# Large tiles moved to multiples of 512 bytes, and the heads' small pool divided in two, in a one-core encoder layer

## The chip, the cores and the metric

The kernel runs on one core of a Trainium2 chip. The metric is device time in microseconds of one execution; 0.2% of it is 3.1 us. A core has TensorE (PE, with its weight loads shown apart as PEld), VectorE (DVE), ScalarE (ACT), GpSimd (POOL) and SyncE (SP), which here issues most DMAs. SBUF is the on-chip memory: 128 partitions, and a tile takes the same bytes at the same address in each of them.

## What is computed

One layer over 1024 tokens of width 1024, all in float32:

```python
h = rmsnorm(x, g_mix)
z = h @ w_in                      # 512 pooling channels | q | k | v, 8 heads
y_pool = pool_mixer(u_pool, w_pool_grp, pool_scale)      # trailing windows 2, 4, 8, 16
y_attn = diff_attention(q, k, v, g_q, g_k, lam, g_sub, lambda_init)   # two softmax maps a head
gates = sigmoid(h @ w_gate + b_gate)
merged = gates[:, :1024] * (y_pool @ w_branch_pool) + gates[:, 1024:] * (y_attn @ w_branch_attn)
x = x + merged @ w_out
h2 = rmsnorm(x, g_ffn)
x = x + square(relu(h2 @ w_up)) @ w_down                 # width 4096 between
```

## The kernel before

**Three matmuls for one.** Every operand is split into a high and a low part in the type fp32r (split, L117): ScalarE copies the value, rounded, into the high part, and VectorE or GpSimd subtracts it from the value into the low part. mm3 (L122) then does hi x hi (L125), hi x lo (L126) and lo x hi (L127). In `matmul(ps, lhs, rhs)` the first operand, lhs, is loaded as weights (128 x 128, so 512 bytes in each partition), and rhs is the one that moves, 512 columns (2048 bytes), or 384, 256 or 128. Nearly every matmul has its own load of weights.

**The stages, in order of time.** The heads (L299 to L674): x is normed and transposed into hT; for each head and each block of 128 tokens, z = hT x wqkv (384 columns), then the preparation of queries and keys, transposes against the identity matrix (L469, L565), the scores sc from Q (weights) and K (moving, L509 and L510), the softmax, its transposed digits AT, and their product with the values, po, and two small products with a matrix of ones (L600, L601). The gates g and the pooling channels u, yp (L677 to L773), computed from hT, are placed by the framework's scheduler between the heads' matmuls. Then the pooling branch bp (L816 to L825), the attention branch ba (L827 to L846), the output projection op (L884), the second norm, and the MLP. The MLP is done with the Strassen-Winograd scheme: w_up in 16 pairs of column blocks, each with seven products of 12 matmuls (up_pair, L1050: X, Y, Z, W from B11, B21, BT1 to BT4 and B22), and w_down in seven products of 192 matmuls (d_product, L1242: Da and Db from u as weights and w moving).

**What sets the order.** Each engine runs its instructions in one fixed order. The framework's scheduler settles it when the program is built, from priorities and its own timeline; loads go out through SP's queue in that order.

**What sets the addresses.** Each `tile_pool` is a stretch of every partition; pools are stacked from the left in the order in which they are opened, or from the right (`side="right"`), and within a pool the tiles follow each other, each rounded up to 32 bytes. The left stack begins at byte 16512. const (L86) lies first and holds the identity identf (512 bytes), mhalf (32), ones (512), inv (64), cols (128) and six more of 32: 1440 bytes. So everything stacked after it begins at 17952, which is 35 x 512 + 32. All tiles from there on are multiples of 512 bytes long, up to the two of fo_tile (L141, 528 floats, 2112 bytes each): after these, fq and up begin at 160 past a multiple of 512. sp (L300), the heads' pool, holds large and small tiles in one: a few of 4 to 64 bytes, then dist, the square sq, qn, the queries' digits Q, oS and oqs. Pools from the right begin at 229344, which is 447 x 512 + 480.

Of the kernel before, what the change touches and what calls it, by code (L numbers as in the profile page):

```python
# [8 lines left out]
F32 = mybir.dt.float32  # L9
F32R = mybir.dt.float32r  # L10
# [7 lines left out]
P = 128  # L18
S = 1024
# [14 lines left out]
N_FW, N_FR, N_FO = 4, 2, 2  # L34
N_Q, N_QN = 3, 2
# [22 lines left out]
def encoder_kernel(  # L58
# [21 lines left out]
    nc = tc.nc  # L80
# [3 lines left out]
    w_up, w_down, w_pool_grp = w_up[0], w_down[0], w_pool_grp[0]  # L84

    const = ctx.enter_context(tc.tile_pool(name="const", bufs=1))  # L86
    dram = ctx.enter_context(tc.tile_pool(name="dram", bufs=1, space=DRAM))
    mix = ctx.enter_context(ExitStack())
    hp0 = [mix.enter_context(tc.tile_pool(name=f"hp0{i}", bufs=4)) for i in "ab"]
# [3 lines left out]
    fp = mix.enter_context(tc.tile_pool(name="fp", bufs=1))  # L93
# [8 lines left out]
    def htile(shape, dt, name, th):  # L102

        if th == 0:
            hcount[0] += 1
        return (hp1 if th else hp0[(hcount[0] - 1) // 4 % 2]).tile(shape, dt, tag="H", name=name)
# [7 lines left out]
    def f(ap):  # L114
        return ap.bitcast(F32)
# [23 lines left out]
        return wpool.tile(shape, F32R, tag="fw", name=name, bufs=N_FW)  # L139

    def fo_tile(name):  # L141
        return fp.tile([P, 528], F32, tag="fo", name=name, bufs=N_FO)

    def fr_tile(shape, name):
        return fp.tile(shape, F32, tag="fr", name=name, bufs=N_FR)
# [88 lines left out]
        mp.append(m)  # L234


    identf = const.tile([P, P], F32, name="identf")
    make_identity(nc, identf)
    mhalf = const.tile([P, NT], F32, name="mhalf")
    nc.gpsimd.memset(mhalf, -0.5)  # L240
    ones = const.tile([P, P], F32R, name="ones")
    nc.gpsimd.memset(f(ones), 1.0)
    inv = const.tile([P, 16], F32, name="inv")
    for i in range(16):
        nc.gpsimd.memset(inv[:, i : i + 1], 1.0 / (i + 1))

    cols = const.tile([P, 32], F32, name="cols")
    gs = const.tile([P, 1], F32, name="gs")
    zero = const.tile([P, 1], F32, name="zero")
    y_dram = dram.tile([D, S], F32, name="y_dram")  # L250
# [10 lines left out]
    def norm_transpose(xt, gb, t, dst, hn, small, banks, halves=False):  # L261

        th, c0 = t // 4, (t % 4) * P
        ss = small.tile([P, 1], F32, tag="ss", name=f"ss{t}", bufs=2)
        rs = small.tile([P, 1], F32, tag="rs", name=f"rs{t}", bufs=2)
        if halves:
            s1 = small.tile([P, 1], F32, tag="ss1", name=f"ss1{t}")
            nc.scalar.activation(hn[:, 0:512], xt[:, 0:512], AF.Square, accum_out=ss)
            nc.vector.tensor_tensor_reduce(
                out=hn[:, 512:D], in0=xt[:, 512:D], in1=xt[:, 512:D],  # L270
                scale=1.0, scalar=D * EPS, op0=ALU.mult, op1=ALU.add, accum_out=s1,
            )
            nc.vector.tensor_scalar(rs, s1, ss, 1.0 / D, op0=ALU.add, op1=ALU.mult)
            nc.gpsimd.tensor_tensor(rs, rs, mhalf[:, 0:1], op=ALU.pow)
        else:
            nc.scalar.activation(hn, xt, AF.Square, accum_out=ss)
            rsq(rs, ss, 1, 1.0 / D)
        for j in range(2):
            js = slice(j * 512, (j + 1) * 512)
            nc.vector.scalar_tensor_tensor(hn[:, js], xt[:, js], rs, gb[:, js], op0=ALU.mult, op1=ALU.mult)  # L280
            trp, trtag = banks[j % len(banks)]
            ps = trp.tile([P, 512], F32, tag=trtag, name=f"hps{t}_{j}")
            for i in range(4):
                k = 4 * j + i
                nc.tensor.transpose(ps[:, i * P : (i + 1) * P], hn[:, k * P : (k + 1) * P], identf)
            for i in range(2):
                kp = 2 * j + i
                src = ps[:, i * 256 : (i + 1) * 256].rearrange("p (a b) -> p a b", a=2)
                split(dst[kp, th, 0][:, :, c0 : c0 + P], dst[kp, th, 1][:, :, c0 : c0 + P], src)
# [7 lines left out]


    with ExitStack() as ph:  # L299
        sp = ph.enter_context(tc.tile_pool(name="sp", bufs=1))  # L300
        ps_s = ph.enter_context(tc.tile_pool(name="ps_s", bufs=N_S, space=PSUM))
        ps_o = ph.enter_context(tc.tile_pool(name="ps_o", bufs=1, space=PSUM))
        ps_t = ph.enter_context(tc.tile_pool(name="ps_t", bufs=N_T, space=PSUM))

        def s1(shape, dt, name, tag, bufs=1):
            return sp.tile(shape, dt, tag=tag, name=name, bufs=bufs)

        xs = {}

# [70 lines left out]
        lqk = s1([P, 4, HD], F32, "lqk", "oq")  # L380
        nc.sync.dma_start(lqk, lambda_qk[0].partition_broadcast(P))

        dist = sp.tile([P, S], F32, name="dist")

        def distances():

# [5 lines left out]
        def columns():  # L392
            cols_ps = ps_t.tile([P, 512], F32, tag="tr", name="cols_ps")
            nc.tensor.transpose(cols_ps[:, 0:32], rows, identf[0:32, 0:32])
            nc.vector.tensor_copy(cols, cols_ps[:, 0:32])
            nc.vector.tensor_scalar(gs, cols[:, 20:21], 1.0 - LAMBDA_INIT, None, op0=ALU.mult)

        def small_params():
# [64 lines left out]
        def stage_qkT(h, t):  # L463

            th, c0 = t // 4, (t % 4) * P
            K, qn = KV[h][0][th], st[h, t]["qn"]
            tr = ps_t.tile([P, 512], F32, tag="tr", name=f"tk{h}_{t}")
            for i in range(2):
                nc.tensor.transpose(  # L469
                    tr[:, i * P : (i + 1) * P], qn[:, 2 * i : 2 * i + 2, :].rearrange("p a b -> p (a b)"), identf  # L470
                )
            Q = sp.tile([P, 2, 2, P], F32R, tag="Q", name=f"Q{h}_{t}", bufs=N_Q)
            halves = (slice(0, HD), slice(HD, P))
            for m in range(2):
                own, other = halves[m], halves[1 - m]
                q, k = tr[own, 0:P], tr[own, P : 2 * P]
                k_hi, q_hi = K[own, m, c0 : c0 + P], Q[own, m, 0, :]
                nc.scalar.copy(k_hi, k)
                nc.vector.tensor_tensor(K[other, m, c0 : c0 + P], k, f(k_hi), op=ALU.subtract)  # L479
                nc.scalar.copy(q_hi, q)  # L480
                nc.vector.tensor_tensor(Q[other, m, 0, :], q, f(q_hi), op=ALU.subtract)
                nc.vector.tensor_tensor(Q[own, m, 1, :], q, f(q_hi), op=ALU.subtract)  # L482
                nc.scalar.copy(Q[other, m, 1, :], q)  # L483
            st[h, t]["Q"] = Q
            yield

        def stage_scores(h, t):

            K, Q = KV[h][0], st[h, t]["Q"]
            n = (t + 1) * P  # L490
# [139 lines left out]
        def stage(w, g):  # L630
            h, t = divmod(g, NT)
            if w == "A":
                if t == 0:
                    head_start(h)
                yield from stage_qkv(h, t)
            elif w == "B":
                yield from stage_prep(h, t)
            elif w == "C":
                yield from stage_qkT(h, t)
            elif w == "D":  # L640
                yield from stage_scores(h, t)
            elif w == "E":
                yield from stage_aT(h, t)
            elif w == "F" and t % 2:
                yield from stage_pv(h, t // 2)
            elif w == "H" and t % 2:
                yield from stage_ssq(h, t // 2)
            elif w == "R" and t == NT - 1:
                yield from stage_norm(h)
            elif w == "W" and t == 0 and h:  # L650
                for kp in range(NK // 2):
                    load_w(h, kp)
                    split_w(h, kp, nc.gpsimd)
# [56 lines left out]
    def pool_group(g):  # L710
# [7 lines left out]
        for th in range(2):  # L718
# [7 lines left out]
            while sh < win:  # L726
                nxt = fo_tile(f"sum{g}_{th}_{sh}")
                nc.gpsimd.tensor_copy(nxt[:, 0:sh], cur[:, 0:sh])
                nc.vector.tensor_tensor(nxt[:, sh:n], cur[:, sh:n], cur[:, 0 : n - sh], op=ALU.add)
                cur = nxt  # L730
                sh *= 2
# [12 lines left out]
            ps = ps_f.tile([P, 512], F32, tag="f", name=f"yp{g}_{th}")  # L744
            mm3(ps, wg[:, 0, :], wg[:, 1, :], m[:, 0, :], m[:, 1, :], True, True)
            yp = fo_tile(f"yps{g}_{th}")
            nc.scalar.activation(yp[:, 0:512], ps, AF.Copy, scale=cols[:, 16 + g : 17 + g])
            nc.scalar.dma_start(p_dram[g * P : (g + 1) * P, th * 512 : (th + 1) * 512], yp[:, 0:512])

    def gate_cols(c):  # L750
        ws = fill_w(w_gate, c * P, f"gate{c}")
        for th in range(2):
            ps = fill_proj(ws, th, f"g{c}_{th}", spare_bank if c >= G_Z else fill_bank)
            fo = fo_tile(f"go{c}_{th}")
            nc.scalar.activation(fo[:, 0:512], ps, AF.Identity, bias=cols[:, c : c + 1])  # L755
            nc.scalar.dma_start(g_dram[c * P : (c + 1) * P, th * 512 : (th + 1) * 512], fo[:, 0:512])
            yield
# [69 lines left out]
    for d in range(NK):  # L827
# [10 lines left out]
        for th in range(2):  # L838
# [5 lines left out]
            t = htile([P, 2, 512], F32R, f"mT{d}_{th}", th)  # L844
# [9 lines left out]
    def pool_of(stack, name, bufs, space=None, side=None):  # L854
        kw = {} if space is None else {"space": space}
        return stack.enter_context(
            tc.tile_pool(name=name, bufs=bufs, reuse_waits="tile", side=side, **kw)
        )
# [7 lines left out]
    dve, pool = nc.vector, nc.gpsimd  # L866
    hs = ctx.enter_context(ExitStack())
    norms = ExitStack()
    nb_pool = pool_of(hs, "nb", 4, side="right")
    pr1 = pool_of(hs, "pr1", N_R1, side="right")  # L870
    pr2 = [pool_of(hs, "pr20", 1, side="right")]
# [460 lines left out]
```

## Time and profile before

| | us |
|---|---|
| median of 3 runs (1557.16 to 1557.71) | 1557.21 |
| the profiled execution's own time | 1556.93 |
| its span, first to last instruction | 1555.1 |
| TensorE busy, 7649 matmuls | 1535.1 |
| VectorE busy | 1012.4 |
| ScalarE busy | 816.0 |
| GpSimd busy | 350.2 |

By start time within the span: heads with gates and pooling channels up to 713 us, the pooling branch up to 746, the attention branch to 835, the output projection with the second norm to about 940, the up stage to 1243, the down stage to 1551. In a row of a view, `L125 PE MATMUL ba<-yT,wba 128*128 128x512` is line, engine, operation, what is written and what is read (the numbers of buffers left out), the array's rows and columns, and the size that moves. A matmul's start is measured, its end is modelled: rows overlap, since the next matmul starts while the one before still runs through the array.

### The profile page before, as it was taken

The numbers are of one execution on the slowest core, as the hardware profiler recorded it, in microseconds if no ns is written. First come the engines' busy times: TensorE is split into PE (matmuls) and PEld (weight loads), VectorE is DVE, ScalarE is ACT, GpSimd is POOL, SyncE is SP. The second block draws the span as 40 slices with busy tenths as digits, with TensorE's granted clock in tenths as the row PEclk, the third lists the DMA queues.
The fourth block names the chain that finished last, engine by engine and source line by source line (L and its number), as shares of the span: only waits on it lengthen the run. The fifth ranks groups of instructions, "written<-read, shape, count | busy, mean of one in ns | idle before, by whom it ended". The sixth has DMA issues, their size and how long they took to land.

```text
span 1555.1 us, 22054 instructions
## 1 busy us (share of the span) xinstructions
PE 1535.1 (99%) x7649; PEld 1321.5 (85%) x7649; DVE 1012.4 (65%) x2268; ACT 816.0 (52%) x1808; POOL 350.2 (23%) x447
## 2 busy tenths in 40 slices
PE   7999999999999999999999999999999999999999
PEld 6999999999998989888888887888888788888887
DVE  6777677777878787765322448766665668556662
ACT  6656556656566556566432456565555634333331
POOL 5433334243425262324453400000000000000000
PEclk9999999999999999999999999999999999999999
DMA  7111212021202031547426524554432789537750
GB/s 229 47 56 48 65 41 68 24 74 40 72 28 84 28 96 42 176 151 235 143 92 198 178 102 122 179 183 159 136 135 109 273 312 385 179 122 256 224 189 27
DMA packets 166681, 206.41 MB, mean 133 GB/s; under 512 B 10069, under 2 KB 102954, under 8 KB 166570
## 3 DMA queue, kind: packets, MB, share of 16 engines
q1 hardware_dynamic: 149162, 177.71, 35.3%
q10 hardware_dynamic: 17408, 27.30, 4.7%
q8 instruction: 60, 0.98, 0.3%
q14 instruction: 51, 0.42, 0.1%
HBM read 150.42 MB, written 54.56 MB: 132 GB/s over the span
## 4 chain that ended last, share of the span: by engine, by line
PE 89%; DVE 4%; issue 2%; DMA 2%; ACT 2%; POOL 1%; POOLq 0%; SPq 0%; ACTq 0%; DVEq 0%
PE z L125 5%; PE z L127 5%; PE z L126 5%; PE Da L126 4%; PE Da L125 4%; PE Da L127 4%; PE g L125 3%; PE g L126 3%; PE g L127 3%; PE Db L126 3%; PE Db L125 3%; PE Db L127 3%; PE X L125 2%; PE X L126 2%; PE X L127 2%; PE sc L509 2%
## 5 line engine op out<-in xcount | busy, mean ns | idle before, releaser
L125 PE MATMUL z<-wqkv,hT 128*128 128x384 f32 x512 | 174.9, 342 | 0.5 <-DVE qn L451 0.3
L127 PE MATMUL z<-wqkv,hT 128*128 128x384 f32 x512 | 174.7, 341 | 0.5 <-DVE hT L120 0.4
L126 PE MATMUL z<-wqkv,hT 128*128 128x384 f32 x512 | 174.0, 340 | 0.0
L520 ACT ACTIVATE s<-s,nm 128x256 f32<-128x256 f32 (+7 forms) x128 | 99.6, 778 | 45.4 <-DVE nm L512 40.7
L259 POOL TENSOR_TENSOR ms<-ms,mhalf 128x4 f32<-128x4 f32 x64 | 66.5, 1040 | 159.0 <-DVE ms L258 140.6
L126 PE MATMUL g<-hT,fwgate 128*128 128x512 f32 x256 | 101.1, 395 | 0.0
L125 PE MATMUL g<-hT,fwgate 128*128 128x512 f32 x256 | 101.0, 394 | 0.1
L127 PE MATMUL g<-hT,fwgate 128*128 128x512 f32 x256 | 101.0, 395 | 0.0
L125 PEld LDWEIGHTS z<-wqkv,hT 128*128 128x128 f32 x512 | 97.1, 190 | 4.3 <-DVE qn L451 1.0
L127 PEld LDWEIGHTS z<-wqkv,hT 128*128 128x128 f32 x512 | 96.9, 189 | 3.1 <-DVE hT L120 1.2
L126 PEld LDWEIGHTS z<-wqkv,hT 128*128 128x128 f32 x512 | 97.1, 190 | 2.9
L512 DVE CUSTOM_DVE_ANT_0 s<-sc,dist 128x512 f32<-128x512 f32 (+3 forms) x128 | 74.6, 586 | 19.5 <-PE sc L510 18.1
L120 POOL TENSOR_TENSOR wqkv<-rqkv,wqkv 128x384 fp32r<-128x384 f32 x60 | 63.7, 1078 | 19.8 <-ACT wqkv L119 19.8
L120 DVE TENSOR_TENSOR AS<-s,AS 128x512 fp32r<-128x512 f32 x64 | 43.9, 688 | 36.1 <-ACT AS L119 35.9
L509 PE MATMUL sc<-K,Q 128*128 128x512 f32 (+2 forms) x192 | 66.8, 354 | 0.1
L510 PE MATMUL sc<-K,Q 128*128 128x512 f32 (+2 forms) x192 | 66.4, 354 | 0.0
L457 POOL TENSOR_TENSOR qn<-qn,ggh 128x128 f32<-128x128 f32 x64 | 32.3, 505 | 138.7 <-DVE qn L451 127.6
L483 ACT CAST Q<-tk 64x128 fp32r<-64x128 f32 x128 | 33.2, 259 | 57.9 <-DVE Q L482 56.0
L480 ACT CAST Q<-tk 64x128 fp32r<-64x128 f32 x128 | 33.0, 258 | 53.5 <-DVE K L479 52.1
L120 POOL TENSOR_TENSOR fwgate<-frgate,fwgate 128x512 fp32r<-128x512 f32 x32 | 43.9, 1376 | 52.3 <-ACT fwgate L119 52.1
L127 PEld LDWEIGHTS g<-hT,fwgate 128*128 128x128 f32 x256 | 48.1, 188 | 8.7
L125 PEld LDWEIGHTS g<-hT,fwgate 128*128 128x128 f32 x256 | 48.2, 188 | 7.4 <-ACT go L755 0.4
(429 smaller groups left out, 4647.0 us busy)
## 6 DMA issues: line engine op xcount, KB each, us to landing
wd<-in_w_down_dram SPq DMA_DIRECT2D x56, 512.0 KB, 5.3
wu<-in_w_up_dram SPq DMA_DIRECT2D x32, 512.0 KB, 5.0
udS<-us SPq DMA_DIRECT2D x64, 256.0 KB, 2.2
ur<-udS SPq DMA_DIRECT2D x32, 512.0 KB, 3.5
rqkv<-in_w_in_dram SPq DMA_DIRECT2D x64, 192.0 KB, 2.8
ud<-u ACTq DMA_DIRECT2D x48, 256.0 KB, 2.9
ur<-ud SPq DMA_DIRECT2D x24, 512.0 KB, 4.9
frgate<-in_w_gate_dram SPq DMA_DIRECT2D x32, 256.0 KB, 2.8
```

Source lines behind the costliest of these rows:

```text
L120: (lo_eng or nc.vector).tensor_tensor(lo, src, f(hi), op=ALU.subtract)
L125: nc.tensor.matmul(ps, lhs_hi, rhs_hi, start=first, stop=False, **kw)
L126: nc.tensor.matmul(ps, lhs_hi, rhs_lo, start=False, stop=False, **kw)
L127: nc.tensor.matmul(ps, lhs_lo, rhs_hi, start=False, stop=last, **kw)
L259: nc.gpsimd.tensor_tensor(dst, dst, mhalf[:, :n], op=ALU.pow)
L457: nc.gpsimd.tensor_tensor(qn[:, 2:4, :], qn[:, 2:4, :], ggh.unsqueeze(1).broadcast_to([P, 2, HD]), op=ALU.mult)
L480: nc.scalar.copy(q_hi, q)
L483: nc.scalar.copy(Q[other, m, 1, :], q)
L509: nc.tensor.matmul(dst, Q[:, i, 0, :], rhs, start=True, stop=False)
L510: nc.tensor.matmul(dst, Q[:, i, 1, :], rhs, start=False, stop=True)
L512: nc.vector.tensor_tensor_reduce(out=s[i][:, c : c + w], in0=sc[:, 0:w], in1=dist[:, o0 + c : o0 + c + w], scale=2.0 ** -(h + 1), scalar=B ...
L520: nc.scalar.activation(s[i][:, 0:n], s[i][:, 0:n], AF.Exp, bias=last, scale=-1.0, accum_out=Z[:, i, t : t + 1])
```

## The change

Nothing is computed otherwise. The changed kernel moves where tiles begin:

- identf and ones leave const for a pool of their own, units, stacked behind it; cols shrinks from 32 to 24 columns (its last 11 were not read). const is then 384 bytes long and ends at 16896, which is 33 x 512; units adds 1024.
- fo_tile's tiles grow from 528 to 576 floats, so that two of them are 9 x 512 bytes.
- sp is divided: sq_pool takes the large tiles (lqk and oq, dist, sq, qn, Q, oS, oqs), sp keeps the small ones and is stacked behind it.
- a tile edge of 480 bytes, written once and never read, is put at the far right, so that the pools from the right begin at a multiple of 512.

```diff
+    units = ctx.enter_context(tc.tile_pool(name="units", bufs=1))
...
     def fo_tile(name):
-        return fp.tile([P, 528], F32, tag="fo", name=name, bufs=N_FO)
+        return fp.tile([P, 576], F32, tag="fo", name=name, bufs=N_FO)
...
-    identf = const.tile([P, P], F32, name="identf")
+    identf = units.tile([P, P], F32, name="identf")
...
-    ones = const.tile([P, P], F32R, name="ones")
+    ones = units.tile([P, P], F32R, name="ones")
...
-    cols = const.tile([P, 32], F32, name="cols")
+    cols = const.tile([P, 24], F32, name="cols")
...
+        sq_pool = ph.enter_context(tc.tile_pool(name="sq", bufs=1))
         sp = ph.enter_context(tc.tile_pool(name="sp", bufs=1))
...
         def s1(shape, dt, name, tag, bufs=1):
-            return sp.tile(shape, dt, tag=tag, name=name, bufs=bufs)
+            return sq_pool.tile(shape, dt, tag=tag, name=name, bufs=bufs)
...
-        dist = sp.tile([P, S], F32, name="dist")
+        dist = s1([P, S], F32, "dist", "dist")
...
-            nc.vector.tensor_copy(cols, cols_ps[:, 0:32])
+            nc.vector.tensor_copy(cols, cols_ps[:, 0:24])
...
-            Q = sp.tile([P, 2, 2, P], F32R, tag="Q", name=f"Q{h}_{t}", bufs=N_Q)
+            Q = s1([P, 2, 2, P], F32R, f"Q{h}_{t}", "Q", N_Q)
...
+    edge = ctx.enter_context(tc.tile_pool(name="edge", bufs=1, side="right"))
+    nc.gpsimd.memset(edge.tile([P, 120], F32, name="edge"), 0.0)
```

The start of each tile, in bytes past a multiple of 512, as the built programs have it (parts of a tile that a matmul reads lie whole multiples of 512 behind its start):

| tiles | read by | before | after |
|---|---|---|---|
| hT, wqkv, fwgate, fwpool, ypT, wbp, wba, wo, mT | z, g, u, bp, ba, op | 32 | 0 |
| A, AS, BT1 to BT4, B22 (up stage) | X, Y, Z, W | 32 | 0 |
| w (down stage, moving) | Da, Db | 32 | 0 |
| K, V, AT, s, x, mix, wgrp, yT | sc, po, ta, yp, ba | 160 | 0 |
| B11, B21 (up stage, moving), y | X, Y, hb | 480 | 0 |
| u (down stage, weights) | Da, Db | 480 | 0 |
| Q and qn | sc, tk | 416 | 0 |
| oqs; ones | po (L600) | 96; 160 | 0; 0 |
| identf | all transposes | 128 | 0 |
| fo's second tile | not by TensorE | 96 | 256 |

No large tile moves by more than 3 KiB, and the order of the stack stays, but for the small tiles of sp, which now lie behind the large ones. On the engines every instruction stands where it stood; GpSimd has one more, the memset of edge, and TensorE waits in two places less for work of its own in the heads' first steps. GpSimd's rows near the start of the program, before (L274 is the first norm's power, L120 the low parts of the first weights):

```order
L372 MEMSET rows 32x128
L274 TENSOR_TENSOR rs_151<-rs_151,mhalf 128x1
L120 TENSOR_TENSOR wqkv_0_191<-rqkv_0_177,wqkv_0_191 128x384
L120 TENSOR_TENSOR wqkv_1_194<-rqkv_0_177,wqkv_1_194 128x384
L120 TENSOR_TENSOR wqkv_4_205<-rqkv_2_183,wqkv_4_205 128x384
```

And in the changed kernel, where L872 is the new line and the other lines have moved by one or two:

```order
L374 MEMSET rows 32x128
L872 MEMSET edge 128x120
L275 TENSOR_TENSOR rs_157<-rs_157,mhalf 128x1
L121 TENSOR_TENSOR wqkv_0_197<-rqkv_0_183,wqkv_0_197 128x384
L121 TENSOR_TENSOR wqkv_1_200<-rqkv_0_183,wqkv_1_200 128x384
```

The memset stands ahead of the first norm's power, although it is written in the MLP's part of the code: it waits for nothing.

## The prediction

> **What bounds the kernel now.** I read the page first, then the stretches of time, and then TensorE's instructions in order of time.
>
> ```profile
> span 1555.1 us, 22054 instructions
> PE 1535.1 (99%) x7649; PEld 1321.5 (85%) x7649; DVE 1012.4 (65%) x2268; ACT 816.0 (52%) x1808; POOL 350.2 (23%) x447
> PEclk9999999999999999999999999999999999999999
> PE 89%; DVE 4%; issue 2%; DMA 2%; ACT 2%; POOL 1%; POOLq 0%; SPq 0%; ACTq 0%; DVEq 0%
> ```
>
> TensorE is busy for 99% of the span at the full granted clock, and the chain that ended last runs over it for 89%. So the time is the number of matmuls times the distance from one start to the next, and that distance is what I look at. The ends of matmuls are modelled (a row of 0.39 us begins every 0.23 us), so I take starts alone. First, stretches of matmuls of 512 columns without a break. Three views in order of time follow, cut to the first and the last row of a stretch: the output projection's first 168 matmuls; then in the MLP's up stage one pair's 60 matmuls of the products 6, 5, 4, 7, 3; then in the attention branch's projection all 384.
>
> ```profile
> 835.62 0.39 PE L125 MATMUL op<-wo,mT 128*128 128x512 f32 x1
> ...
> 873.48 0.40 PE L127 MATMUL op<-wo,mT 128*128 128x512 f32 x1
> ```
> ```profile
> 1176.00 0.39 PE L125 MATMUL X<-BT2h,AS 128*128 128x512 f32 x1
> ...
> 1189.40 0.39 PE L127 MATMUL Z<-B22h,AS 128*128 128x512 f32 x1
> ```
> ```profile
> 746.02 0.40 PE L125 MATMUL ba<-yT,wba 128*128 128x512 f32 x1
> ...
> 835.39 0.39 PE L127 MATMUL ba<-yT,wba 128*128 128x512 f32 x1
> ```
>
> The first gives 37.86 us over 167 distances, 226.7 ns; the second 13.40 over 59, 227.1 ns; the third 89.37 over 383, 233.3 ns. It is the same instruction on the same shape, and no wait lies in any of them: in the stretches of time TensorE is busy throughout.
>
> ```profile
> core 0: us, PE busy (x), PEclk, DMA share, GB/s
> 747.00:835.00 88.00, 88.00 (x379) 1.00 0.34 108
> 836.00:873.00 37.00, 37.00 (x165) 1.00 0.80 239
> 1250.00:1550.00 300.00, 300.00 (x1313) 1.00 0.62 213
> ```
>
> Two more stretches are slow: a pair's products 1 and 2 (24 matmuls), and the whole down stage (7 products of 192, 1344 matmuls).
>
> ```profile
> 1189.62 0.39 PE L125 MATMUL X<-B11h,A 128*128 128x512 f32 x1
> ...
> 1194.99 0.39 PE L127 MATMUL Y<-B21h,A 128*128 128x512 f32 x1
> ```
> ```profile
> 1243.50 0.39 PE L125 MATMUL Da<-w_0h,u_0h 128*128 128x512 f32 x1
> ...
> 1550.90 0.39 PE L127 MATMUL Da<-w_7h,u_7l 128*128 128x512 f32 x1
> ```
>
> That is 5.37 us over 23, 233.5 ns, and 307.40 over 1343, 228.9 ns.
>
> What tells the slow from the fast is where their operands lie. By the table of offsets above, both operands of the output projection (wo, mT) and of the products on BT and B22 lie 32 bytes past a multiple of 512. In the slow three the two differ: yT at 160 against wba at 32; B11 and B21 at 480 against A at 32; w at 32 against u at 480. In the groups over the whole run each (columns: busy us, mean ns of one) the same step shows:
>
> ```profile
> L125 PE MATMUL bp<-ypT,wbp 128*128 128x512 f32 x64 | 25.0, 390 | 0.0
> L125 PE MATMUL X<-BT2h,AS 128*128 128x512 f32 x64 | 25.0, 390 | 0.0
> L125 PE MATMUL ba<-yT,wba 128*128 128x512 f32 x128 | 50.6, 395 | 0.0
> L126 PE MATMUL X<-B11l,A 128*128 128x512 f32 x64 | 25.3, 395 | 0.0
> ```
>
> Equal offsets take 390, unequal ones 395. My reading: while a matmul streams its moving operand, the weights of the next are read, and the two streams hinder each other where they are out of step within a line.
>
> **The change part by part.** The large tiles' offsets all become 0, so every pair above becomes an equal one. I price an equal pair at 226.7 ns, the output projection's distance.
>
> - Attention branch: 384 x (233.3 - 226.7) = 2.5 us.
> - Up stage, products 1 and 2: 16 pairs x 24 = 384 matmuls x (233.5 - 226.7) = 2.6 us.
> - Down stage: 1344 x (228.9 - 226.7) = 3.0 us.
>
> All three lie on the path itself, since TensorE waits for nothing there. The sum is 8.1 us. What would be late next is the loads of the down stage: DMA is busy for 0.62 of it, and TensorE's demand grows by 1%, so nothing.
>
> Is it the absolute offset that counts, so that 0 is better or worse than an equal 32? The trace has no large operand at 0, but it has equal pairs at two places: the scores' product with the values has both operands at 160, the heads' projection both at 32.
>
> ```profile
> 689.59 0.28 PE L126 MATMUL po<-AT_0l,V 128*128 128x256 f32 x1
> ...
> 692.22 0.28 PE L127 MATMUL po<-AT_4h,V 128*128 128x256 f32 x1
> ```
> ```profile
> 400.21 0.34 PE L125 MATMUL z<-wqkv,hT 128*128 128x384 f32 x1
> ...
> 404.20 0.34 PE L127 MATMUL z<-wqkv,hT 128*128 128x384 f32 x1
> ```
>
> 2.63 us over 22 distances is 119.5 ns for 256 columns at 160; 3.99 over 23 is 173.5 for 384 columns at 32. With 226.7 for 512 that is a straight line of (226.7 - 119.5) / 256 = 0.42 ns a column and some 13 ns on top of each matmul, whether the offset is 32 or 160. So I take an equal pair at 0 to cost what one at 32 does.
>
> The stages in which heads and gates interleave (up to 713 us) hold equal and unequal groups in turn:
>
> ```profile
> L125 PE MATMUL z<-wqkv,hT 128*128 128x384 f32 x512 | 174.9, 342 | 0.5 <-DVE qn L451 0.3
> L125 PE MATMUL g<-hT,fwgate 128*128 128x512 f32 x256 | 101.0, 394 | 0.1
> L509 PE MATMUL sc<-K,Q 128*128 128x512 f32 x96 | 38.8, 404 | 0.1
> L510 PE MATMUL sc<-K,Q 128*128 128x512 f32 x96 | 37.9, 395 | 0.0
> ```
>
> The gates' matmuls are an equal pair and still take 394 where bp takes 390. What they have and bp has not is a change of shape every few matmuls, and that stays. I take nothing for these stages. The bounds: nothing below, and above 768 x 4 ns for the gates, 192 x 10 for the scores (the mean of 404 and 395 less 390), 5.0 us; then 16 returns from B21 to BT2 in the up stage with a few slow matmuls each, a fraction of 1 us.
>
> For the other engines I look for the same copy at different offsets: u from 480 to 480, w from 480 to 32, yT from 32 to 160, fwgate from 32 to 32.
>
> ```profile
> L119 ACT CAST u_5h<-ur 128x1024 fp32r<-128x1024 f32 x7 | 7.3, 1048 | 25.5 <-PE Da L126 11.4 <-issue 7.1 <-PE Db L126 7.0
> L119 ACT CAST w_5h<-wd 128x1024 fp32r<-128x1024 f32 x5 | 5.2, 1047 | 0.0
> L119 ACT CAST yT<-ry 128x512 fp32r<-128x512 f32 x16 | 9.2, 621 | 3.0 <-DVE ry L214 1.8 <-DVE s L529 1.0 <-DMA r_dram<-rT 0.2
> L119 ACT CAST fwgate<-frgate 128x512 fp32r<-128x512 f32 x32 | 19.8, 618 | 6.6 <-PE g L127 3.0 <-DMA frgate<-in_w_gate_dram 2.9 <-issue 0.6
> ```
>
> They agree within 0.5%: nothing for ScalarE, and VectorE and the DMAs I put at nothing as well, since they have room beside a TensorE at 99%. Edits with one answer: the new memset on GpSimd costs about what that of rows does, 0.19 us, in 3.45 us of idle time; the copy of cols gets narrower, off the path; no other instruction changes its place.
>
> ```profile
> 1.93 0.19 POOL L372 MEMSET rows<- 32x128 f32 x1
> 5.58 0.56 POOL L274 TENSOR_TENSOR rs<-rs,mhalf 128x1 f32<-128x1 f32 x1 [3.45 <-DVE rs L273]
> ```
>
> The profiled execution took 1556.93 us (1555.1 of span and 1.8 around it), 0.3 under the median of 1557.21. 1556.9 - 8.1 = 1548.8, against the median 1549.1.
>
> **The rivals.** *Nothing changes.* The fast groups' tiles all start below byte 131072 of a partition, and in the slow groups one operand lies above 158000 and the other below. If it is the region and not the offset that slows them, the change moves no tile to another region, and the time stays at 1557.2. For it: products 1 and 2 and the attention branch, with offsets 128 and 448 apart, have the same 233 ns. Against it: down has its operands as far apart and only 228.9, and hT and the heads' weights, up to 95 thousand bytes apart, keep the 173.5. The Trainium skill, TensorE: Matmul & The Clock Gate, Step-by-step: what each phase is for, says that moving operand and weights have read ports of their own and that loading the next weights takes nothing from a running matmul. By that rule no offset between the two would count, and the time would stay too; 233.3 against 226.7 ns without a wait speaks against the rule as it stands. Chance 0.14.
>
> *Far more is gained.* All large offsets before are odd multiples of 32. If the 13 ns on top of each matmul are themselves the price of starting off a line, they go: some 7100 matmuls (7649 less the transposes) x 13 ns = 92 us, and the time could be as low as 1457; a part of it is as possible. Against it stands that shifting an equal pair from 32 to 160 left the 13 ns alone. The same page, in its part on 56 against 53.3 ns, has a fixed 2.5 ns on a warm matmul; by it some 10 of the 13 would be open to gain, as an estimate, and no run here shows such a matmul. Chance 0.10 for over 8 us beyond the forecast.
>
> *Slower.* With every tile at a line's start, streams that were spread over five offsets (32, 96, 160, 416, 480) begin at the same place: in the heads and gates ScalarE, VectorE and GpSimd write tiles while TensorE reads others. If that makes TensorE's matmuls there as slow as the unequal pairs (6.6 ns more), 3360 matmuls (1536 z, 768 g, 192 u, 384 sc, 480 po) cost 22.2 us, and the time is 1557.2 - 8.1 + 22.2 = 1571. It turns the sign from 8.1 us / 3360 = 2.4 ns a matmul. Against it: z, whose operands lie at 32, kept its 173.5 while ScalarE and GpSimd wrote the gates' and heads' weights at 32 as well. Chance 0.06.
>
> **How the numbers follow.** The forecast has 0.70: 1549.1 us, in its own range from 1552 (if down stays as it is) to 1541 (with the bounds of heads, gates and returns and 2 us for what I see no row for). What a measurement of this kernel can tell from no change is about 0.2%, 3.1 us. The range reaches up to the second case, 1557.8, and leaves out the large gain and the loss (0.16). Faster: the forecast and the large gain, 0.80; within 0.2%: 0.14; slower: 0.06.
>
> **What would show it.** In the profile after, the mean of ba, of X<-B11 and Y<-B21 and of Da and Db falls to that of bp, BT and op, 389 to 390, and the down stage's 1344 matmuls take 304.7 us and not 307.6; bp, op and BT stay. If ba keeps 395 while all offsets are 0, the offset was not the cause. If bp and z themselves fall, the absolute offset counts and the forecast is too small. If z and g rise, the third rival holds.

## The result and the profile after

The changed kernel takes 1548.49 us (median of 6 runs, 1548.34 to 1549.08); in the same rounds the kernel before takes 1557.43 (6 runs, 1557.16 to 1558.01). The ratio is 0.9943, 95% interval 0.9930 to 0.9955: faster by 0.6%, where 0.2% can be told. The forecast was 1549.1.

The page of the changed kernel, whose profiled execution took 1548.34 us:

```profile
span 1546.6 us, 22053 instructions
PE 1526.0 (99%) x7649; PEld 1320.4 (85%) x7649; DVE 1012.4 (65%) x2268; ACT 816.5 (53%) x1808; POOL 350.9 (23%) x448
PE 91%; DVE 3%; issue 2%; ACT 1%; DMA 1%; POOL 1%; SPq 1%; POOLq 0%; DVEq 0%; ACTq 0%
```

TensorE has the same 7649 matmuls and still fills 99% of a span that is 8.5 us shorter. The other engines' busy times moved by less than 1 us. So nothing was taken off the path, and matmuls follow each other faster. Stretches of time as before (columns: window, length, PE busy with its matmuls, granted clock, DMA share, GB/s):

```profile
747.00:835.00 88.00, 88.00 (x390) 1.00 0.35 112
836.00:873.00 37.00, 37.00 (x169) 1.00 0.68 221
1250.00:1540.00 290.00, 290.00 (x1281) 1.00 0.62 216
```

The first holds 390 matmuls where it held 379, though part of that is that the output projection now begins inside it. The starts tell it without that. First and last row of the attention branch, of one pair's products 1 and 2, and of the down stage, in TensorE's order of time:

```profile
745.22 0.39 PE L126 MATMUL ba<-yT,wba 128*128 128x512 f32 x1
...
832.04 0.39 PE L128 MATMUL ba<-yT,wba 128*128 128x512 f32 x1
...
1184.32 0.39 PE L126 MATMUL X<-B11h,A 128*128 128x512 f32 x1
...
1189.54 0.39 PE L128 MATMUL Y<-B21h,A 128*128 128x512 f32 x1
...
1237.95 0.39 PE L126 MATMUL Da<-w_0h,u_0h 128*128 128x512 f32 x1
...
1542.36 0.39 PE L128 MATMUL Da<-w_7h,u_7l 128*128 128x512 f32 x1
```

86.82 us over 383 distances, 5.22 over 23 and 304.41 over 1343 are 226.7, 227.0 and 226.7 ns, where 233.3, 233.5 and 228.9 stood before. In the groups over the whole run (columns: busy us, mean ns of one, idle before):

```profile
L126 PE MATMUL z<-wqkv,hT 128*128 128x384 f32 x512 | 174.5, 341 | 0.4 <-DVE qn L453 0.3
L126 PE MATMUL g<-hT,fwgate 128*128 128x512 f32 x256 | 101.0, 395 | 0.1
L126 PE MATMUL op<-wo,mT 128*128 128x512 f32 x128 | 50.3, 394 | 0.0
L126 PE MATMUL ba<-yT,wba 128*128 128x512 f32 x128 | 49.8, 389 | 0.0
L127 PE MATMUL X<-B11l,A 128*128 128x512 f32 x64 | 25.0, 391 | 0.0
L126 PE MATMUL bp<-ypT,wbp 128*128 128x512 f32 x64 | 25.0, 391 | 0.0
L126 PE MATMUL Da<-w_0h,u_0h 128*128 128x512 f32 x32 | 12.4, 389 | 0.0
```

ba and X have come down from 395 to bp's 389 to 391; z, g, op and bp stand where they stood. By stage, from the first matmul of one to the first of the next:

| stage | before | after | difference | forecast |
|---|---|---|---|---|
| up to the first z | 10.92 | 10.59 | -0.3 | 0 |
| heads and gates, first z to first bp | 691.46 | 690.95 | -0.5 | 0 |
| pooling branch | 43.64 | 43.68 | 0.0 | 0 |
| attention branch | 89.60 | 87.04 | -2.6 | -2.5 |
| output projection, second norm | 93.36 | 93.40 | 0.0 | 0 |
| up stage | 314.52 | 312.29 | -2.2 | -2.6 |
| down stage, first to last start | 307.40 | 304.41 | -3.0 | -3.0 |

### The profile page after: what moved, and what is told of

Same layout as the page of the kernel before. It is cut to its first block, busy times and chain, and to the rows that moved or that the text cites. A ratio compares the mean times of both kernels' runs of the same rounds, so it can differ in the third digit from the quotient of the medians.

```text
span 1546.6 us, 22053 instructions
## 1 busy us (share of the span) xinstructions
PE 1526.0 (99%) x7649; PEld 1320.4 (85%) x7649; DVE 1012.4 (65%) x2268; ACT 816.5 (53%) x1808; POOL 350.9 (23%) x448
## 4 chain that ended last, share of the span: by engine, by line
PE 91%; DVE 3%; issue 2%; ACT 1%; DMA 1%; POOL 1%; SPq 1%; POOLq 0%; DVEq 0%; ACTq 0%
PE z L126 5%; PE z L128 5%; PE z L127 5%; PE Da L126 4%; PE Da L127 4%; PE Da L128 4%; PE g L126 3%; PE g L127 3%; PE g L128 3%; PE Db L126 3%; PE Db L127 3%; PE Db L128 3%; PE X L126 2%; PE X L128 2%; PE X L127 2%; PE sc L512 2%
## 5 line engine op out<-in xcount | busy, mean ns | idle before, releaser
L126 PE MATMUL z<-wqkv,hT 128*128 128x384 f32 x512 | 174.5, 341 | 0.4 <-DVE qn L453 0.3
L128 PE MATMUL z<-wqkv,hT 128*128 128x384 f32 x512 | 174.1, 340 | 0.0
L127 PE MATMUL z<-wqkv,hT 128*128 128x384 f32 x512 | 173.8, 339 | 0.0
L126 PE MATMUL g<-hT,fwgate 128*128 128x512 f32 x256 | 101.0, 395 | 0.1
L127 PE MATMUL g<-hT,fwgate 128*128 128x512 f32 x256 | 101.0, 395 | 0.0
L128 PE MATMUL g<-hT,fwgate 128*128 128x512 f32 x256 | 101.0, 395 | 0.0
L126 PEld LDWEIGHTS z<-wqkv,hT 128*128 128x128 f32 x512 | 96.8, 189 | 3.9 <-DVE qn L453 1.0
L127 PEld LDWEIGHTS z<-wqkv,hT 128*128 128x128 f32 x512 | 96.6, 189 | 3.0
L128 PEld LDWEIGHTS z<-wqkv,hT 128*128 128x128 f32 x512 | 96.6, 189 | 2.2 <-DVE hT L121 0.5
L128 PEld LDWEIGHTS g<-hT,fwgate 128*128 128x128 f32 x256 | 48.1, 188 | 8.6
L126 PEld LDWEIGHTS g<-hT,fwgate 128*128 128x128 f32 x256 | 48.2, 188 | 7.3 <-ACT go L757 0.4
```

The lines of the kernel that those rows point to most:

```text
L126: nc.tensor.matmul(ps, lhs_hi, rhs_hi, start=first, stop=False, **kw)
L127: nc.tensor.matmul(ps, lhs_hi, rhs_lo, start=False, stop=False, **kw)
L128: nc.tensor.matmul(ps, lhs_lo, rhs_hi, start=False, stop=last, **kw)
```

## The experiments

**What was to be told apart.** The theory: what counts is the difference of the two operands' starts, and equal starts are the cheap case, wherever they lie. Its rivals: it is the start on a line itself (the absolute offset) that was gained; it is which memory region a tile lies in; or the gain came with the divided pool of the heads. All kernels are the changed kernel with one edit. "Offset" below is the start of the moving operand minus that of the weights, in bytes. Some expectations count in cycles: a cycle there is a column's time, 0.42 ns, and "on top" means beyond one cycle for each of the 512 columns (an equal pair has 32 cycles, 13 ns). The distances of the down stage and of the attention branch are means over the whole of them. Those of the shorter runs (products 1 and 2, the gates, z) are means within runs of one shape and one pair of offsets, without the first seven matmuls of each run.

**all160: everything equal, but off the line.**

```diff
+    pad = units.tile([P, 40], F32, name="pad")
+    nc.gpsimd.memset(pad, 0.0)
...
-    nc.gpsimd.memset(edge.tile([P, 120], F32, name="edge"), 0.0)
+    nc.gpsimd.memset(edge.tile([P, 80], F32, name="edge"), 0.0)
```

> The changed kernel with every large tile 160 bytes past a multiple of 512 in place of 0, so that nothing starts on a line but all pairs stay equal. Theory 1 (what counts is the difference between the offset of the moving operand and that of the weights being loaded): as the changed kernel, 1548.5 us within 1.5, ba, X, Y, Da and Db at 389 to 391. Rival (what counts is that an operand starts at the line, or that 160 itself is a bad offset for a moving one): the 384 matmuls of ba return to 395 (2.5 us more), and with the same 6.6 ns on all 5900 matmuls of 384 and 512 columns some 39 us more, 1587.

Measured: 1548.93 us (5 runs, 1548.38 to 1549.46), ratio to before 0.9949 (0.9936 to 0.9961). Its down stage:

```profile
1237.98 0.39 PE L126 MATMUL Da<-w_0h,u_0h 128*128 128x512 f32 x1
...
1542.39 0.39 PE L128 MATMUL Da<-w_7h,u_7l 128*128 128x512 f32 x1
```

304.41 us, the same as at 0. With every large tile at 160 past a line the whole gain is there: it isn't the line, it is that the two are equal.

**right64: the signed swap.** The pools from the right begin at 64. B11 and B21 then move 64 ahead of A, and u as weights lies 64 ahead of the moving w.

```diff
-    nc.gpsimd.memset(edge.tile([P, 120], F32, name="edge"), 0.0)
+    nc.gpsimd.memset(edge.tile([P, 104], F32, name="edge"), 0.0)
```

> The changed kernel with the pools from the right 64 bytes past a multiple of 512 (B11, B21 and the down stage's u at 64, all else at 0). Before, B11 and B21 stood 64 short of their weights and the down stage's u 64 short of w; now they stand 64 beyond. Theory 1 with a sign (moving less weights): the two stages change places against before, X and Y on B11 and B21 take what the down stage took (228.9 ns, 0.8 us more in all), the down stage 233.4 (9.0 us more), together 1558.3 us. Rival without a sign (only the distance of 64 counts, and the stage sets its size): both as before, 233.5 and 228.9, 5.6 us more, 1554.1. Rival of the region (which half of the memory an operand lies in): no change, 1548.5.

Measured: 1558.94 us (11 runs, 1557.92 to 1560.54), ratio 1.0015 (1.0006 to 1.0023): all of the gain of the MLP is gone and more. One pair's products 1 and 2, and the down stage:

```profile
1185.85 0.40 PE L126 MATMUL X<-B11h,A 128*128 128x512 f32 x1
...
1191.13 0.39 PE L128 MATMUL Y<-B21h,A 128*128 128x512 f32 x1
...
1239.59 0.40 PE L126 MATMUL Da<-w_0h,u_0h 128*128 128x512 f32 x1
...
1552.95 0.39 PE L128 MATMUL Da<-w_7h,u_7l 128*128 128x512 f32 x1
```

313.36 us over 1343 is 233.3 ns for the down stage, which had 228.9 before; over all 16 pairs, products 1 and 2 have 228.8 where they had 233.3 (the pair shown has 5.28 us over 23, 229.6, its first seven matmuls included). The two stages have changed places, though the tiles of the right side lie only 416 bytes, and the left ones only 32, from where they lay before. That refutes the region of memory as the cause, and it shows that the sign of the offset counts: before, X and Y moved 448 ahead, which is 64 behind the next line, and down moved 64 ahead of it.

**fo528: one term by itself.** fo's tiles go back to 528 floats, so that yT (with K, V, AT and the queries' digits) lies 128 past the line and wba on it.

```diff
-        return fp.tile([P, 576], F32, tag="fo", name=name, bufs=N_FO)
+        return fp.tile([P, 528], F32, tag="fo", name=name, bufs=N_FO)
```

> One part undone: the two tiles of fo_tile are 528 floats again, so that everything stacked behind them up to the end of the heads' pools lies at 128 and all else at 0. Theory 1: only ba has unequal operands in bulk (yT at 128, wba at 0), the same difference as before, 395 and 2.5 us more, 1551.0; the heads keep their time, since K, Q, V and AT are all at 128. Rival (the heads' interleaved stage is hurt by groups at two offsets): more than 1553.

Measured: 1551.68 us (7 runs, 1550.79 to 1553.81), ratio 0.9969 (0.9957 to 0.9980).

```profile
745.67 0.40 PE L126 MATMUL ba<-yT,wba 128*128 128x512 f32 x1
...
835.04 0.39 PE L128 MATMUL ba<-yT,wba 128*128 128x512 f32 x1
```

89.37 us over 383 again, 233.3 ns, while its down stage keeps 304.42. The attention branch's 2.6 us hang on this pair alone; of the other 0.6 between the two medians, 0.45 is there before the branch begins (745.67 against 745.22).

**heads_undone: the divided pool put back.** identf and ones return to const, and the heads' large tiles to the mixed pool sp.

```diff
-    units = ctx.enter_context(tc.tile_pool(name="units", bufs=1))
...
-    identf = units.tile([P, P], F32, name="identf")
+    identf = const.tile([P, P], F32, name="identf")
...
-    ones = units.tile([P, P], F32R, name="ones")
+    ones = const.tile([P, P], F32R, name="ones")
...
-        sq_pool = ph.enter_context(tc.tile_pool(name="sq", bufs=1))
...
-            return sq_pool.tile(shape, dt, tag=tag, name=name, bufs=bufs)
+            return sp.tile(shape, dt, tag=tag, name=name, bufs=bufs)
```

> One part undone: the heads' small pool in one again, identity and ones back in const, all else as in the changed kernel: Q and qn at 256, ones at 160, oqs at 448, identity at 128. Theory 1: 192 scores of 512 columns, 64 of 384 and 128 of 256 have unequal operands, at most 6.6 ns each, but they never run more than two in a row and are in the middle of changes of shape anyway: 0 to 1.5 us more, 1548.5 to 1550. Rival (the division carries a good part of the gain): 3 us or more, over 1551.5.

Measured: 1549.27 us (5 runs, 1548.82 to 1550.60), ratio 0.9952 (0.9940 to 0.9965), 0.8 us above the changed kernel with overlapping intervals. Heads and gates take 691.67 us from the first z to the first bp; nine kernels whose heads are those of the changed kernel, or those shifted by a constant, spread from 690.40 (right192) to 691.88 (right128), and before has 691.46. So the divided pool carries nothing that these runs can tell, and the 0.5 us in the table above is within the spread. As the next runs show, this kernel was a weak test: Q lies 256 past the line in it and K on it, and 256 turned out to be as good as equal; before, 416 and 160, it was the same.

**right32, right128, right192, right256, right96: the offset as a scale.** The same edit as right64's, with an edge of 112, 88, 72, 56 and 96 floats, as here for the first:

```diff
-    nc.gpsimd.memset(edge.tile([P, 120], F32, name="edge"), 0.0)
+    nc.gpsimd.memset(edge.tile([P, 112], F32, name="edge"), 0.0)
```

> Pools from the right at 32, all else at 0: X and Y on B11, B21 have the moving operand 32 ahead of the weights, the down stage 32 behind. If operands are fetched in pieces of 64 bytes or more and only the piece counts: 226.7 ns in both, 1548.6 us. If every byte of difference counts: both between 226.7 and the values at 64 (228.8 and 233.3), 1549 to 1558.

> Pools from the right at 128. X and Y on B11, B21 (moving 128 ahead) take what ba took before with the same difference, 233.3 ns, 2.5 us more. The down stage (moving 128 behind) is open: if the pattern repeats every 256 bytes, 128 behind is 128 ahead, 233.3, 8.9 us more and 1560.0 in all; if it repeats only every 512, something else between 226.7 and 240.

> Pools from the right at 192. If the pattern repeats every 256 bytes, 192 ahead is 64 behind: X and Y 233.3 (2.5 us), the down stage 228.8 (2.8 us), 1553.9 in all. If it repeats every 512, neither value is known and they need not be these.

> Pools from the right at 256. If the pattern repeats every 256 bytes, this is an equal pair: 226.7 in both stages, 1548.6 us, and 512 in the change could have been 256. If it repeats every 512, this is the farthest apart that two offsets can be, and both stages are slower than 226.7: up to 1560 or more.

> The changed kernel with a tile edge of 384 bytes and not 480: the pools from the right begin 96 bytes past a line. B11 and B21 (moving) are 96 ahead of A, u (weights) 96 ahead of w. Of distances modulo 256, +32, +128 and -32, -64, -128 have given 46 to 48 cycles on top of the columns, +64 37, 0 32; +96 and -96 are unknown. Guess: 48 in both, 384 x 6.7 + 1344 x 6.7 = 11.5 us, 1560.0. If it goes with the distance from 64, as +64 is cheap, +96 lies between 37 and 48: 1558 to 1560.

Measured: right32 1560.51 us (8 runs, ratio 1.0021, 1.0009 to 1.0032); right128 1558.47 (8 runs, 1.0007, 0.9995 to 1.0018); right192 1554.13 (8 runs, 0.9981, 0.9969 to 0.9992); right256 1549.40 (3 runs, 0.9950, 0.9928 to 0.9973); right96 1562.16 (5 runs, 1.0032, 1.0019 to 1.0045). Each fence holds the down stage of one kernel, first right32, then right128, right192, right256 and right96:

```profile
1240.68 0.39 PE L126 MATMUL Da<-w_0h,u_0h 128*128 128x512 f32 x1
...
1554.05 0.40 PE L128 MATMUL Da<-w_7h,u_7l 128*128 128x512 f32 x1
```
```profile
1240.60 0.41 PE L126 MATMUL Da<-w_0h,u_0h 128*128 128x512 f32 x1
...
1552.69 0.39 PE L128 MATMUL Da<-w_7h,u_7l 128*128 128x512 f32 x1
```
```profile
1239.88 0.39 PE L126 MATMUL Da<-w_0h,u_0h 128*128 128x512 f32 x1
...
1547.28 0.39 PE L128 MATMUL Da<-w_7h,u_7l 128*128 128x512 f32 x1
```
```profile
1239.02 0.39 PE L126 MATMUL Da<-w_0h,u_0h 128*128 128x512 f32 x1
...
1543.43 0.39 PE L128 MATMUL Da<-w_7h,u_7l 128*128 128x512 f32 x1
```
```profile
1240.83 0.39 PE L126 MATMUL Da<-w_0h,u_0h 128*128 128x512 f32 x1
...
1555.47 0.39 PE L128 MATMUL Da<-w_7h,u_7l 128*128 128x512 f32 x1
```

313.37, 312.09, 307.40, 304.41 and 314.64 us over 1343 distances. With products 1 and 2 of the same kernels, the kernel before and the ones above, all eight multiples of 32 within 256 bytes are there (512 columns; the offset modulo 256):

| offset | ns | from |
|---|---|---|
| 0 | 226.7 | down of after, all160 and right256 (-256) |
| 32 | 233.3 | X, Y of right32 |
| 64 | 228.8 to 228.9 | X, Y of right64; down of before and of right192 (-192) |
| 96 | 233.3 | X, Y of right96 |
| 128 | 232.4 to 233.3 | ba of before and fo528; X, Y and down of right128 |
| 160 | 234.3 | down of right96 (-96) |
| 192 | 233.3 | X, Y of before and of right192; down of right64 (-64) |
| 224 | 233.3 | down of right32 (-32) |

Two readings that I had brought are corrected by this. The pattern repeats after 256 bytes, not 512: right256 is as fast as equal starts. And the distance isn't a measure: 32 is as bad as 192, only 64 ahead is cheap, some 2.1 ns on top of the equal pair where the rest have 5.7 to 7.6. With it, right32 missed both of its cases: 1560.51 us, where they ended at 1558. The guess for right96 was 48 cycles for both and 1560.0 us; the moving operand 96 behind has 50.3 (234.3 ns), the worst found, and the total is 2.2 us higher. No offset beats the equal one.

**weights32: do the heads and gates pay at all?** hT, ypT and mT stay on the line, and what they meet goes to 32.

```diff
     hp1 = mix.enter_context(tc.tile_pool(name="hp1", bufs=8))
+    gap = mix.enter_context(tc.tile_pool(name="gap", bufs=1))
+    nc.gpsimd.memset(gap.tile([P, 8], F32, name="gap"), 0.0)
     wpool = mix.enter_context(tc.tile_pool(name="wpool", bufs=1))
```

> The changed kernel, with a 32-byte tile between the tiles of hT, ypT and mT (they stay at 0) and the weights and values that they meet (wqkv, fwgate, wbp, wba, wo, K, V, AT, yT, which go to 32). It asks whether the interleaved heads and gates pay for unequal pairs at all, since the change showed almost nothing there. Equal pairs stay in ba, the scores and the MLP. Theory 1 (the relative offset counts for every matmul, in runs and between changes of shape alike): z, g and u go from 32 to 48 cycles on top, 2496 x 6.6 ns = 16.5 us; bp 192 x 6.6 = 1.3 and op 384 x 6.6 = 2.5 as well: 1548.5 + 20.3 = 1568.8. Theory 2 (it counts only in long runs of one shape; where the shape changes every few matmuls something else ends later): bp and op still pay 3.8, the heads nothing: 1552.3. In between is likely, since z comes 24 in a row: 1536 x 6.6 = 10.1 for z alone, 1562. In the instruction order, some steps from the second norm on are scheduled otherwise than in the changed kernel, so that the heads are read from their own stage time (701.5 us up to the first bp in the changed kernel).

Measured: 1561.88 us (6 runs, 1560.77 to 1562.05), ratio 1.0031 (1.0019 to 1.0043). The total comes near one of the forecast values, and that is a coincidence. Its groups:

```profile
L128 PE MATMUL z<-wqkv,hT 128*128 128x384 f32 x512 | 175.4, 343 | 0.5 <-DVE qn L455 0.3
L128 PE MATMUL g<-hT,fwgate 128*128 128x512 f32 x256 | 101.7, 397 | 0.1
L128 PE MATMUL op<-wo,mT 128*128 128x512 f32 x128 | 50.8, 398 | 0.0
L128 PE MATMUL bp<-ypT,wbp 128*128 128x512 f32 x64 | 25.4, 397 | 0.0
```

bp and op, in long runs, pay in full (233.3 ns in their steady parts). z, g and u pay only a part: heads and gates take 694.02 us, 3.1 more than in the changed kernel, against the 16.5 of theory 1. The mean distance of the gates' matmuls grows by 2.3 ns and that of the pooling channels' (u) by 3.2, not 6.6, and z's by 0.4. The gates and u pay little because most of their runs are short: from the eighth matmul of a run on they have 233.2 ns where they had 227.0 and 226.8, which is nearly the full price. z is another case: even from the eighth matmul on it has 174.6 ns where it had 173.5. So with 384 columns the same offset costs 1.1 ns, with 512 it costs 6.6. Of the other 10.3 us, bp has 1.2 and 0.3 is net in the stretch of the output projection. 8.9 lie in the up stage, where no offset is changed. The waits of TensorE there, of this kernel, then stretches of its time (the granted clock stands behind the count of matmuls) and two matmuls:

```profile
PE Z L128 <- ACT BT1h L122: 3.4, 1, 3.4
PE hb L945 <- ACT y L1010: 2.1, 1, 2.1
```
```profile
930.00:954.00 24.00, 20.53 (x99) 1.00 0.22 67
954.30:964.40 10.10, 6.68 (x15) 0.50 0.27 89
964.50:1000.00 35.50, 35.50 (x158) 1.00 0.70 210
```
```profile
959.53 0.63 PE L129 MATMUL Y<-B21l,A 128*128 128x512 f32 x1
959.96 0.63 PE L130 MATMUL Y<-B21h,A 128*128 128x512 f32 x1
```

The scheduler placed the steps from the second norm on otherwise. All waits of the stage come to 9.0 us against 4.7 in the changed kernel, 4.3 more. From 954.2 to 964.5 us the granted clock is 0.50, where the changed kernel has 1.00 in every stretch of this stage; some 15 matmuls of 512 columns follow each other at about 430 ns in it, not 227, which makes 3.0 us. And 16 transposes of about 0.1 us, which the changed kernel has ahead of the up stage, stand inside it here: 1.6 us. Together these are the 8.9. That is a cost of the order, not of an offset, and the 13.4 us between the medians must not be read as the price of 32 bytes. That the waits brought the lower clock is likely, since it comes among them, but no run tests it. The profiles of all160, fo528, ul32, right32 and right256 show the clock at 0.50 as well, for 3.4 us near the start of the up stage; those of the kernel before and of the changed kernel don't. It hardly moves the stage there: all160 has 312.42 us against 312.29, and the wait for A that the changed kernel has (0.8 us) is gone.

**q64: the scores made unequal.**

```diff
+        nc.gpsimd.memset(s1([P, 16], F32, "padq", "padq"), 0.0)
```

> The changed kernel, with a 64-byte tile ahead of sq, qn, Q, oS and oqs: the queries' digits Q (weights of the scores) begin 64 bytes past a line, K (moving) on it; oqs and the ones are 64 apart as well. Before, Q and K were 256 bytes apart, which the last runs showed to be an equal pair, so that this is the first kernel in which the scores are unequal. Order unchanged. Theory 1 (the relative offset counts in the heads too): 384 scores x 6.6 ns = 2.5 us, 1551.0, and the mean distance within the scores' groups 6.6 ns longer. Theory 2 (between changes of shape nothing is paid): 1548.5. The scores come in groups of a few between transposes and products, so that I expect 0.5 to 2.

Measured: 1549.05 us (4 runs, 1548.66 to 1549.73), ratio 0.9950 (0.9933 to 0.9967). Its scores:

```profile
L512 PE MATMUL sc<-K,Q 128*128 128x512 f32 x96 | 38.9, 405 | 0.1
L513 PE MATMUL sc<-K,Q 128*128 128x512 f32 x96 | 38.1, 397 | 0.0
```

The changed kernel has 403 and 396. The mean distance from a score of 512 columns to the next start is 238.8 ns, in the changed kernel 238.0; with the narrower ones that is 0.3 us for all 384 scores, if it is a difference at all. Its heads and gates take 692.16 us, 1.2 more than in the changed kernel and 0.3 above the spread of the nine kernels named above, so that 1.2 us is the most that the stage allows. Groups of one or two matmuls between other shapes pay little.

**ul32: whose weights?** In the down stage the low parts of u lie 32 before the line, all the rest on it. Of the three matmuls of a step only the third (L128) has u's low part as its weights, and only beside the second (L127) is it loaded.

```diff
-    puo = pool_of(ctx, "puo", 8, side="right")
+    puh = pool_of(ctx, "puh", 4, side="right")
+    gap = pool_of(ctx, "gap", 1, side="right")
+    nc.gpsimd.memset(gap.tile([P, 8], F32, name="gap"), 0.0)
+    pul = pool_of(ctx, "pul", 4, side="right")
...
-        for n, src, pool_ in (("u", ur, puo), ("w", second(j, q), pwo)):
-            hi, lo = (pool_.tile([P, 2, 512], F32R, tag="op", name=f"{n}{j}_{q}{x}") for x in "hl")
+        for n, src, pools in (("u", ur, (puh, pul)), ("w", second(j, q), (pwo, pwo))):
+            hi, lo = (p_.tile([P, 2, 512], F32R, tag="op", name=f"{n}{j}_{q}{x}") for p_, x in zip(pools, "hl"))
```

> The changed kernel, but in the down stage the low parts of u lie in a pool of their own, 32 bytes before the line (480), and the high parts and w stay on the line. Of three matmuls of one step (high x high, high x low, low x high) only the third has its own weights out of step with its moving operand, and only during the second are weights out of step loaded, since the next matmul's weights are loaded while one runs. Theory 'the weights to come': the distance from the second to the third start is 233.3 ns, the others 226.7. Theory 'its own weights': the distance from the third to the next first is 233.3, the others 226.7. Either way a third of 1344 matmuls pays, 448 x 6.6 = 3.0 us: 1551.5. If it is neither, both distances rise, or all three by a third of it. At the seam of up and down some steps are scheduled otherwise, so that the distances in the down stage carry the answer, not the total.

Measured: 1558.02 us (10 runs, 1555.53 to 1560.84), ratio 1.0007 (0.9997 to 1.0016). The down stage, and one step of it in order of time with the loads of weights (PEld) beside the matmuls:

```profile
1239.70 0.39 PE L126 MATMUL Da<-w_0h,u_0h 128*128 128x512 f32 x1
...
1300.25 0.39 PE L127 MATMUL Db<-w_2l,u_2h 128*128 128x512 f32 x1
1300.25 0.19 PEld L128 LDWEIGHTS Db<-w_2h,u_2l 128*128 128x128 f32 x1
1300.48 0.40 PE L128 MATMUL Db<-w_2h,u_2l 128*128 128x512 f32 x1
1300.48 0.19 PEld L126 LDWEIGHTS Db<-w_3h,u_3h 128*128 128x128 f32 x1
1300.72 0.39 PE L126 MATMUL Db<-w_3h,u_3h 128*128 128x512 f32 x1
...
1550.08 0.40 PE L128 MATMUL Da<-w_7h,u_7l 128*128 128x512 f32 x1
```

310.38 us over 1343 distances, 231.1 ns: 6.0 us more than in the changed kernel, twice the 3.0 that either theory gave. (The profiled execution took 1556.07 us; why the median of the ten is 2.0 us above it isn't known.) By line, over 448 steps, the distance to the next start is 228.3 after L126, 229.2 after L127 and 235.8 after L128 (226.8, 226.3 and 226.9 without the edit). The groups show it too:

```profile
L128 PE MATMUL Da<-w_0h,u_0l 128*128 128x512 f32 x32 | 12.7, 397 | 0.0
L127 PE MATMUL Da<-w_0l,u_0h 128*128 128x512 f32 x32 | 12.6, 393 | 0.0
L126 PE MATMUL Da<-w_0h,u_0h 128*128 128x512 f32 x32 | 12.5, 390 | 0.0
```

Neither forecast holds as it stands. The excess is 13.3 ns a step, twice 6.7: as if two matmuls of the three paid, the one beside which these weights are loaded and the one that uses them. Of it 8.9 come after the start of the matmul that uses them; "the weights to come", the reading of the prediction, would have put all at L127. But a single distance is not quite the price of its matmul: where all pairs are unequal, long and short distances take turns (229 and 237 ns in ba of the kernel before). The Trainium skill, Perfetto Trace Analysis, Per-instruction lifecycle, has the recorded start of a matmul as the moment at which it begins to fetch its operand, not that at which the array begins on it; if so, a delay of the array shows in a later row, and no run here can tell by how many. What is firm is the sum. Which of the two streams hinders the other, and where, stays open. The span is 7.7 us longer than the changed kernel's: these 6.0, and 1.7 in the up stage, at whose end some steps are scheduled otherwise and TensorE's longest wait is 3.2 us and not 1.6.

## Why the prediction was right, point by point

- **The bound.** TensorE's chain of starts, and its distances without a wait: right. Shorter distances are 2.6 + 2.5 + 3.0 = 8.1 of the 8.5 us by which the span fell.
- **Attention branch**, 2.5: measured 2.6, and fo528 takes it back alone.
- **Down stage**, 3.0: measured 3.0. It was the smallest step a matmul (2.2 ns) and the largest term, since it has 1344 of them.
- **Up stage**, 2.6: measured 2.2. The distances fell as forecast, 16 pairs x 24 x (233.5 - 227.0) = 2.5 us; the sum took the equal pair at 226.7 there. The other 0.3 went into waits: the stage's four waits of TensorE (for U, BT1h, u and A) are there before and after, and three of them are 0.1 us longer.
- **An equal pair at 0 costs what one at 32 does:** right, and all160 adds 160: 226.7 in all three.
- **Heads and gates at nothing:** right within the spread of the runs, but its reason was not the one that counted. There was next to nothing unequal to mend: z, g, u and po were equal pairs before, by the table of offsets, and the scores, which it took for an unequal pair, lay 256 apart, which is as good as equal. That changes of shape hide an offset, its own reason, holds for short groups (q64) and only in part for the gates (weights32).
- **The new memset and the other engines at nothing:** no term is left over for them; the three stages are 7.8 of the 8.5 us of span, and the rest lies in the start and the heads, in amounts that kernels with the same heads differ by. So it is partly luck that the total came within 0.6 us of the forecast: the stages gave 0.3 less, and the start and the heads 0.8 that it had put at nothing.
- **The mechanism behind the price** was called a reading: two streams out of step within a line while the next weights are read. That the relative offset is the cause is shown, by all160 and right64 above all. The line of 512 bytes is wrong, it repeats after 256; and "the next weights" alone is not what ul32 shows. Where the two streams meet stays open.
- **The rivals.** Nothing changes (the region): refuted by the result and by right64. Beside it stood a rule of the Trainium skill, TensorE: Matmul & The Clock Gate, Step-by-step: what each phase is for: the two operands have read ports of their own, and a load takes nothing from a running matmul. If no offset between the two counted by that rule, as the prediction read it, these runs contradict it: 32 bytes of shift cost 6.7 ns a matmul. Far more is gained: the 13 ns on top of each matmul are there at 0, 32 and 160 alike, so they are not the price of starting off a line; what they are wasn't tried. Slower: z and g have 341 and 395 where they had 342 and 394, so common starts of many streams did no harm.

## What to carry to other kernels

Where a profile shows one engine full, compare the distances of equal instructions in stretches without a wait; a step between them is worth as much as a wait, and it may come from where operands lie. For back-to-back matmuls with a load of weights each (in fp32r, the one type tried), let the moving operand and the weights start equally modulo 256 bytes: moving the bases of the pools did that here, with a pad tile where one was needed, and absolute alignment did nothing. Look for it in runs of more than some seven wide matmuls; short groups of changing shapes pay little. And take a granted clock from short windows: over 930 to 960 us weights32 shows a mean of 0.90, and it was 1.00 and then 0.50.

## What the runs showed of the hardware that was not expected

- The price of an offset repeats after 256 bytes, has a sign (64 ahead 2.1 ns, 64 behind 6.7), and isn't graded by distance.
- It depends on the columns: at an offset of 32, 6.6 ns with 512 columns and 1.1 with 384 (weights32).
- Putting one of three weights out of step costs two thirds of the price of all three and not one third: 13.3 ns a step of three matmuls (ul32).
- It is hardly paid in the first matmuls of a run among other shapes, and nearly whole from the eighth on: 233.2 ns in the gates against 227.0 (weights32).
- Among some 7 us of waits at the start of the up stage the granted clock fell to 0.50 for 10.2 us and was 1.00 again after it (weights32); matmuls of 512 columns then begin 430 ns apart.
